# Masked copies of two chunks' score products in one instruction

## The chip, the cores and the metric

The kernel runs on one core of one Trainium2 chip, as one launch. The metric is the device time of that launch in microseconds (us), a median over several executions. The engines are called PE (TensorE, matrix products; PEld is its weight load), DVE (VectorE), ACT (ScalarE), POOL (GpSimd) and SP (SyncE, which here only issues DMAs).

## The reference, cut to what matters

Two blocks in a row. The second (a conformer convolution and a squared-relu MLP) is untouched. The first projects 1024 tokens of 1024 values, runs two kinds of gated linear attention (4 heads "G" with 256 value columns, 4 heads "H" with 128) and a cross-attention to 256 memory rows, gates the result and projects it back. The change lies in the gated linear attention:

```python
def chunked_gated_linear_attention(q, k, v, log_g):
    """Causal recurrence S_t = diag(g_t) S_{t-1} + k_t v_t^T, o_t = S_t^T q_t, chunkwise."""
    ...
    causal = jnp.tril(jnp.ones((CHUNK, CHUNK), dtype=bool))[:, :, None]
    diff = bcum[..., :, None, :] - bcum[..., None, :, :]
    decay = jnp.where(causal, jnp.exp(jnp.where(causal, diff, 0.0)), 0.0)
    scores = jnp.einsum('bhnid,bhnjd,bhnijd->bhnij', qf, kf, decay)
    o_intra = jnp.einsum('bhnij,bhnjv->bhniv', scores, vf)
    chunk_kv = jnp.einsum('bhncd,bhncv->bhndv', kf * jnp.exp(b_last - bcum), vf)
    ...
    o_inter = jnp.einsum('bhncd,nbhdv->bhncv', qf * jnp.exp(bcum), states_prev)
    return (o_intra + o_inter).reshape(b_, h_, s_, dv)
```

## The kernel before, in words

The first block works on the sequence in two halves of 512 tokens. In each half it handles 8 units (G heads singly, H heads and cross-attention heads in pairs). A unit's projections are large products on PE, split in three passes (high by high, high by low, low by high); they are the main work, and a task of them consists of groups that write the PSUM tile `ps_d`. The gated attention of a head in one half of the sequence is called a pass here; there are 16 passes (8 heads, 2 halves), all between about 70 and 1005 us. A pass has 4 chunks of 128 tokens, handled as two pairs (0, 1) and (2, 3).

For a pair `cc`, `scores(cc, half)` in `chunk_steps` makes the transposed score matrix of each chunk, a 128x128 tile `at`, from products of keys and queries at eleven levels of a binary tree: the diagonal, and blocks of 1, 2, 4, 4 columns (half 0) and of 8, 16, 16, 32, 64, 64 (half 1). Each half makes four products of 192 columns on PE: two groups `g` of operands, for each of the two chunks `m`. Before, a PSUM tile `p[m]` holds the two groups of one chunk, and the copies into `at` are made chunk by chunk in turn: `copy_predicated` takes from PSUM, where a byte mask is set, into every second block of columns. So a pair has 10 copies in half 0 and 12 in half 1, 704 in all. There are four `at` tiles, used in turn.

Then `turn(cc)` transposes the keys (`K` to `kT`), and `output(c)` multiplies a chunk's `at` with the values (in the trace `ps_m<-v,at`), adds the product of queries and state, and makes the state's update (`ps_m<-v,kT`). The steps of a pass stand in the order sc(0,0), sc(0,1), tu(0), sc(2,0), ou(0), sc(2,1), ou(1), tu(2), ou(2), ou(3). The PSUM tiles of scores (`ps_s`), of transposes and of outputs (`ps_m`) share one ring of 5 banks, so a product can wait for the bank of an earlier one.

What else is on DVE: the factors before the products (`a`, `Q`, `q`, `tree`), the low parts of the weights (`wlo`, shared with POOL by a rule in `rest`), the sums of the modulation (`macc`), and adding the output projection to the residual (`xl`).

**The order is written by a planner** while the program is built. It keeps a model of every engine's time (class `Model`), emits the groups of the big products one by one, and between two of them (`service`) emits every step that it holds to be due: whose inputs (`need`) and banks (`banks`) are ready by the model no later than PE's own modelled time plus 0.05. The model counts for each operand tile the stretch of memory it touches, so it knows which copies wait for which. Nothing is reordered at run time: each engine executes its list in order. Nearly every instruction is recorded through one helper, so its line is L217.

Of the kernel before, what the change touches and what calls it, by code (L numbers as in the profile page):

```python
# [10 lines left out]
F32 = mybir.dt.float32  # L11
# [8 lines left out]
P = 128  # L20
# [339 lines left out]
def block_kernel(ctx, tc, x, mem, w_in, w_up, w_kv, w_out, w_mod, w_pw1, w_pw2, w_dw, w_1, w_2,  # L360
# [3 lines left out]
    V, A, G, PE, DMA = [Engine(e, n, M) for e, n in ((nc.vector, "DVE"), (nc.scalar, "ACT"), (nc.gpsimd, "POOL"),  # L364
                                                     (nc.tensor, "PE"), (nc.sync, "DMA"))]
# [12 lines left out]
    def pt(tag):  # L378
        ring, bufs = BANKS[tag]
        p = ps.tile([P, 512], F32, tag=ring, name="ps_" + tag, bufs=bufs)  # L380
        M.alloc(ring, bufs, p)
        return p
# [64 lines left out]
    msk = pc.tile([P, 768], U8, name="msk")  # L447
# [1 line left out]
    lbt = pc.tile([P, 16], F32, name="lbt")  # L449
    first_only = ctx.enter_context(ExitStack())  # L450
    pb = first_only.enter_context(tc.tile_pool(name="pb", bufs=1))
    at = [pb.tile([P, P], F32, name=f"at{i}") for i in range(4)]
    for a in at:
        G.memset(a, 0.0)
    state = {}
# [214 lines left out]
    def blocks(ap, n):  # L670
        return ap.rearrange("p (b n) -> p b n", n=n)

    def factor_steps(u, j, f, req, ev):

        def up(h):
# [72 lines left out]
    n_at = [0]  # L748

    def chunk_steps(t, kind, h, u, j, f, req, ev, soon=None):  # L750
# [3 lines left out]
        st = state[kind, h]  # L754

        def scores(cc, half):
            cs = [slice(c * P, (c + 1) * P) for c in (cc, cc + 1)]
            if half == 0:
                for c in (cc, cc + 1):
                    f["at", c] = at[n_at[0] % len(at)]  # L760
                    n_at[0] += 1
            lv = ((u[f"k{j}"], u[f"q{j}"]), (f["K2"], f["Q2"])) if half == 0 else ((f["K8"], f["Q8"]), (f["K32"], f["Q32"]))
            p = [pt("s"), pt("s")]
            for m in range(2):
                for g, (ks, qs) in enumerate(lv):
                    PE.matmul(p[m][:, 192 * g:192 * (g + 1)], ks[:, cs[m]], qs[:, cc + m], start=True, stop=True)
            a = [f["at", cc], f["at", cc + 1]]
            if half == 0:
                for m in range(2):
                    V.copy_predicated(a[m], msk[:, :P], p[m][:, :P])  # L770
            col = 128 if half == 0 else 384
            for hh in (1, 2, 4, 4) if half == 0 else (8, 16, 16, 32, 64, 64):
                o = col - 384 * half
                for m in range(2):
                    V.copy_predicated(blocks(a[m], 2 * hh)[:, :, hh:], blocks(msk[:, col:col + 64], hh),
                                      blocks(p[m][:, o:o + 64], hh))
                col += 64

        def turn(cc):
            cs = [c for c in (cc, cc + 1) if not (t == NHALF - 1 and c == NT - 1)]  # L780
            p = pt("m")
            for m, c in enumerate(cs):
                PE.transpose(p[:, m * P:(m + 1) * P], f["K128"][:, c * P:(c + 1) * P], ident)
            kt = pb.tile([P, 2, P], F32, tag="kT", name="kT", bufs=2)
            A.copy(kt[:, :len(cs), :], p[:, :len(cs) * P].rearrange("p (m c) -> p m c", c=P))
            f["kT", cc], f["kT", cc + 1] = kt[:, 0, :], kt[:, 1, :]
# [27 lines left out]
        def sc(cc, half):  # L814
            names = ("K2", "Q2") if half == 0 else ("K8", "Q8", "K32", "Q32")
            return Step(lambda: scores(cc, half), lambda: [f[n] for n in names] + [f["at", c] for c in (cc, cc + 1) if half], 2)
# [954 lines left out]
    def put(name, steps, rank):  # L1771
        for st in steps:
            st.rank = rank
        lanes[name] += steps
# [4 lines left out]
    for s_, (t, (kind, h)) in enumerate(units):  # L1779
        u = us[s_]  # L1780
        if kind == "G":
            f = {}
# [10 lines left out]
        elif kind == "H":  # L1793
            for j in range(2):
                f = {}
# [6 lines left out]
        else:  # L1802
            f = [{}, {}]
            a, b = [cross_steps(u, 2 * h + j, j, f[j], [("in", s_, "q"), ("kv", 3)]) +
                    finish_steps(kind, u, j, f[j], ("mix", s_) if j else None) for j in range(2)]
# [228 lines left out]
def build(nc, arrays, dbg=None):  # L2034
    aps = [nc.dram_tensor(f"in_{n}_dram", arrays[n].shape, mybir.dt.from_np(arrays[n].dtype), kind="ExternalInput").ap()
           for n in _ARGS]
    out = nc.dram_tensor("out_0_dram", (S, D), F32, kind="ExternalOutput").ap()
    with tile.TileContext(nc) as tc:
        block_kernel(tc, *aps, out, dbg=dbg)
# [11 lines left out]
```

## Time and profile before

| what | value |
|---|---|
| median of 3 runs | 2040.17 us (2037.25 to 2045.69) |
| the profiled execution's own time | 2043.66 us |
| its span | 2041.6 us |
| PE busy | 1952.8 us, 96% |
| DVE busy | 1504.7 us, 74% |
| ACT busy | 919.5 us, 45% |
| POOL busy | 811.9 us, 40% |
| PE's mean granted clock | 0.987 of full |

How to read it: the span is the stretch from the first to the last instruction in the profile; the execution's own time is a little longer. An engine that is busy 96% of the span bounds the kernel; what the others do counts where PE waits for them. A duration in the trace runs from an instruction's start to the acknowledgement of its last write, so the instructions of one engine may overlap by a little.

### The profile page before, as it was taken

The page shows a single profiled execution, that of the slowest core. Times are in us where ns is not written, and L with a number is a line of the kernel's source. Part 1 is how long each engine was busy: PE and PEld are TensorE (multiplying, and loading weights), DVE is VectorE, ACT ScalarE, POOL GpSimd, SP SyncE. Part 2 cuts the span into 40 slices and gives each one's busy share as a digit, 9 for nine tenths or more (in the row PEclk, how much of TensorE's full clock was granted, in tenths as well). Part 3 has the DMA queues.
Part 4 walks back from the last instruction along what each step waited for, and adds up shares of the span by engine and source line. Part 5 has one row for each costly group of instructions (what it writes and reads, how often), then busy time and mean ns, then how long its engine had stood idle before and what let it go on. Part 6 is the DMA issues. An engine that isn't in the chain of part 4 may idle for free.

```text
span 2041.6 us, 29949 instructions
## 1 busy us (share of the span) xinstructions
PE 1952.8 (96%) x10892; PEld 1699.0 (83%) x10892; DVE 1504.7 (74%) x2956; ACT 919.5 (45%) x1793; POOL 811.9 (40%) x743
## 2 busy tenths in 40 slices
PE   8999999999999998999899999999999998899998
PEld 6888898789788887878789999997878886688786
DVE  5799777744667877856757676887888778777876
ACT  6433333444623334334424343335777776433343
POOL 3343334344333443343536343650000003877872
PEclk9999999999999999999999999999999999999999
DMA  5242331333123332322433232331699899776765
GB/s 198 68 159 104 114 114 63 144 124 105 45 101 136 123 109 89 133 83 83 141 133 119 71 119 91 117 132 62 179 300 270 245 263 300 264 285 263 268 250 204
DMA packets 177638, 315.05 MB, mean 154 GB/s; under 512 B 9762, under 2 KB 129442, under 8 KB 163794
## 3 DMA queue, kind: packets, MB, share of 16 engines
q1 hardware_dynamic: 175186, 309.33, 44.8%
q10 hardware_dynamic: 2304, 3.80, 0.5%
q8 instruction: 86, 1.41, 0.3%
q14 instruction: 62, 0.51, 0.1%
HBM read 241.78 MB, written 71.31 MB: 153 GB/s over the span
## 4 chain that ended last, share of the span: by engine, by line
PE 64%; DVE 20%; ACT 5%; DMA 4%; issue 3%; POOL 3%; SPq 0%; DVEq 0%; POOLq 0%; ACTq 0%
PE ps_d L217 38%; PE ps_s L217 20%; PE ps_m L217 7%; DVE macc L217 2%; DVE Q L217 2%; DVE wlo L217 2%; DMA sl<-so 1%; DVE a L217 1%; DVE at L217 1%; DVE tree L217 1%; DMA wlo<-sl 1%; DVE xn L217 1%; POOL wlo L217 1%; DVE zt L217 1%; DVE actl L217 1%
## 5 line engine op out<-in xcount | busy, mean ns | idle before, releaser
L217 POOL TENSOR_TENSOR wlo<-wst,whi 128x512 fp32r<-128x512 f32 (+1 forms) x235 | 335.9, 1444 | 393.0 <-ACT whi L217 387.9
L217 PE MATMUL ps_d<-hTh,whi 128*128 128x512 f32 x576 | 234.7, 407 | 0.0
L217 PE MATMUL ps_d<-hTh,wlo 128*128 128x512 f32 x576 | 227.8, 395 | 0.0
L217 PE MATMUL ps_d<-hTl,whi 128*128 128x512 f32 x576 | 227.5, 395 | 0.0
L217 PE MATMUL ps_d<-whi,acth 128*128 128x256 f32 x768 | 219.4, 286 | 0.5 <-DVE yg L217 0.5
L217 PE MATMUL ps_d<-wlo,acth 128*128 128x256 f32 x768 | 218.3, 284 | 1.2 <-POOL wlo L217 1.2
L217 POOL TENSOR_TENSOR wst<-wst,g 128x512 f32<-128x512 f32 x64 | 93.3, 1476 | 317.0 <-DMA g<-g2d 291.4
L217 PE MATMUL ps_d<-whi,actl 128*128 128x256 f32 x768 | 217.9, 284 | 0.0
L217 ACT CAST whi<-wst 128x1024 fp32r<-128x1024 f32 (+1 forms) x182 | 189.5, 1049 | 48.7 <-PE ps_d L217 42.9
L217 PE MATMUL ps_s<-tm,whi 128*128 128x512 f32 x620 | 191.9, 391 | 5.9 <-ACT ps_s L217 3.2
L217 PE MATMUL ps_s<-hm,tw 128*128 128x512 f32 x768 | 183.1, 393 | 5.5 <-ACT hc L217 3.4
L217 PEld LDWEIGHTS ps_s<-hm,tw 128*128 128x128 f32 x768 | 144.4, 189 | 38.5 <-ACT hc L217 5.3
L217 DVE TENSOR_TENSOR wlo<-wst,whi 128x512 fp32r<-128x512 f32 (+1 forms) x133 | 109.6, 837 | 66.4 <-ACT whi L217 63.3
L217 PEld LDWEIGHTS ps_d<-wlo,acth 128*128 128x128 f32 x768 | 148.0, 193 | 2.0 <-POOL wlo L217 1.7
L217 PEld LDWEIGHTS ps_d<-whi,acth 128*128 128x128 f32 x768 | 148.0, 193 | 1.0 <-issue 1.0
L217 PEld LDWEIGHTS ps_d<-whi,actl 128*128 128x128 f32 x768 | 148.1, 193 | 0.0
L217 PEld LDWEIGHTS ps_s<-tm,whi 128*128 128x128 f32 x620 | 115.6, 188 | 32.7 <-ACT ps_s L217 5.0
L217 DVE COPY_PREDICATED at<-msk,ps_s 128x64 f32<-128x64 uint8 (+1 forms) x704 | 109.2, 245 | 37.1 <-PE ps_s L217 37.0
L217 PEld LDWEIGHTS ps_d<-hTh,whi 128*128 128x128 f32 x576 | 110.3, 191 | 24.3 <-issue 3.3
L217 PEld LDWEIGHTS ps_d<-hTh,wlo 128*128 128x128 f32 x576 | 109.9, 191 | 24.2
L217 PEld LDWEIGHTS ps_d<-hTl,whi 128*128 128x128 f32 x576 | 110.2, 191 | 21.6 <-issue 0.2
L217 PE MATMUL ps_s<-tm,wlo 128*128 128x512 f32 x310 | 121.1, 391 | 4.6 <-DMA wlo<-sl 4.6
(290 smaller groups left out, 4995.3 us busy)
## 6 DMA issues: line engine op xcount, KB each, us to landing
wst<-in_w_in_dram SPq DMA_DIRECT2D x46, 1024.0 KB, 4.8
wst<-in_w_dram SPq DMA_DIRECT2D x32, 1024.0 KB, 6.7
sh<-so SPq DMA_DIRECT2D x112, 256.0 KB, 4.2
sl<-so SPq DMA_DIRECT2D x112, 256.0 KB, 4.0
whi<-sh SPq DMA_DIRECT2D x31, 896.0 KB, 4.8
wlo<-sl SPq DMA_DIRECT2D x31, 896.0 KB, 7.5
wm<-in_w_mod_dram SPq DMA_DIRECT2D x48, 512.0 KB, 6.8
wst<-in_w_pw_dram SPq DMA_DIRECT2D x24, 1024.0 KB, 4.9
```

The source lines that it names most:

```text
L217: r = f(*args, **kw)
```

## The change

The products of one group for both chunks now lie side by side in one bank (`p[g]`, 192 columns for each chunk), and are made group by group. The scores of both chunks of a pair lie in one tile `at` of 128 x 2 x 128; there are two such tiles instead of four single ones. `put` masks both chunks with one `copy_predicated`, the mask being read twice through a broadcast. The first copy of half 0 (the diagonal) and the blocks of 1 come from the first bank, the others of half 0 from the second; in half 1 the blocks 8, 16, 16 come from the first bank and 32, 64, 64 from the second.

```diff
--- before.py
+++ after.py
@@ -449,7 +449,7 @@
     lbt = pc.tile([P, 16], F32, name="lbt")
     first_only = ctx.enter_context(ExitStack())
     pb = first_only.enter_context(tc.tile_pool(name="pb", bufs=1))
-    at = [pb.tile([P, P], F32, name=f"at{i}") for i in range(4)]
+    at = [pb.tile([P, 2, P], F32, name=f"at{i}") for i in range(2)]
     for a in at:
         G.memset(a, 0.0)
     state = {}
@@ -670,6 +670,9 @@
     def blocks(ap, n):
         return ap.rearrange("p (b n) -> p b n", n=n)
 
+    def blocks4(ap, n):
+        return ap.rearrange("p m (b n) -> p m b n", n=n)
+
     def factor_steps(u, j, f, req, ev):
 
         def up(h):
@@ -754,27 +757,36 @@
         st = state[kind, h]
 
         def scores(cc, half):
-            cs = [slice(c * P, (c + 1) * P) for c in (cc, cc + 1)]
             if half == 0:
-                for c in (cc, cc + 1):
-                    f["at", c] = at[n_at[0] % len(at)]
-                    n_at[0] += 1
+                a = at[n_at[0] % len(at)]
+                n_at[0] += 1
+                for m in range(2):
+                    f["at", cc + m] = a[:, m, :]
+                f["at2", cc] = a
+            a = f["at2", cc]
             lv = ((u[f"k{j}"], u[f"q{j}"]), (f["K2"], f["Q2"])) if half == 0 else ((f["K8"], f["Q8"]), (f["K32"], f["Q32"]))
             p = [pt("s"), pt("s")]
-            for m in range(2):
-                for g, (ks, qs) in enumerate(lv):
-                    PE.matmul(p[m][:, 192 * g:192 * (g + 1)], ks[:, cs[m]], qs[:, cc + m], start=True, stop=True)
-            a = [f["at", cc], f["at", cc + 1]]
+            for g, (ks, qs) in enumerate(lv):
+                for m in range(2):
+                    PE.matmul(p[g][:, 192 * m:192 * (m + 1)], ks[:, (cc + m) * P:(cc + m + 1) * P], qs[:, cc + m], start=True, stop=True)
+
+            def put(dst, col, n, v, o, w):
+                mk = msk[:, col:col + n]
+                if w < n:
+                    mk, v = blocks(mk, w), blocks4(v[:, :, o:o + n], w)
+                    mk = mk.unsqueeze(1).to_broadcast([P, 2, n // w, w])
+                else:
+                    mk, v = mk.unsqueeze(1).to_broadcast([P, 2, n]), v[:, :, o:o + n]
+                V.copy_predicated(dst, mk, v)
+            v = [p[g][:, :384].rearrange("p (m t) -> p m t", m=2) for g in range(2)]
             if half == 0:
-                for m in range(2):
-                    V.copy_predicated(a[m], msk[:, :P], p[m][:, :P])
-            col = 128 if half == 0 else 384
+                put(a, 0, P, v[0], 0, P)
+            col, o = (128, 128) if half == 0 else (384, 0)
             for hh in (1, 2, 4, 4) if half == 0 else (8, 16, 16, 32, 64, 64):
-                o = col - 384 * half
-                for m in range(2):
-                    V.copy_predicated(blocks(a[m], 2 * hh)[:, :, hh:], blocks(msk[:, col:col + 64], hh),
-                                      blocks(p[m][:, o:o + 64], hh))
+                dst = blocks4(a, 2 * hh)[:, :, :, hh:] if hh < 64 else a[:, :, hh:]
+                put(dst, col, 64, v[o // 192], o % 192, hh)
                 col += 64
+                o += 64
 
         def turn(cc):
             cs = [c for c in (cc, cc + 1) if not (t == NHALF - 1 and c == NT - 1)]
```

The change moves instructions too, since the planner sees other tiles and other sizes. The number of products (PE), of ACT's and of SP's instructions stays the same; 704 copies become 352 (320 of 128 columns, 32 of 256), and seven `wlo` subtractions go from POOL to DVE. Behind some 1005 us the order is as before. Three places, the first on DVE, in the first pass, half 0 of the first pair, with what each instruction waits for (PE_49 is PE's semaphore, DVE_49 is DVE's own). Before, two tiles (`at_122`, `at_123`) in turn:

```order
L217 COPY_PREDICATED at_122<-msk,ps_s 128x128 [waits PE_49]
L217 COPY_PREDICATED at_123<-msk,ps_s 128x128 [waits PE_49]
L217 COPY_PREDICATED at_122<-msk,ps_s 128x64 [waits DVE_49]
L217 COPY_PREDICATED at_123<-msk,ps_s 128x64 [waits DVE_49]
L217 COPY_PREDICATED at_122<-msk,ps_s 128x32x2 [waits DVE_49]
L217 COPY_PREDICATED at_123<-msk,ps_s 128x32x2 [waits DVE_49]
L217 COPY_PREDICATED at_122<-msk,ps_s 128x16x4 [waits DVE_49]
```

and of the change, all on one tile:

```order
L217 COPY_PREDICATED at_122<-msk,ps_s 128x256 [waits PE_49]
L217 COPY_PREDICATED at_122<-msk,ps_s 128x128 [waits DVE_49]
L217 COPY_PREDICATED at_122<-msk,ps_s 128x64x2 [waits DVE_49,PE_49]
L217 COPY_PREDICATED at_122<-msk,ps_s 128x32x4 [waits DVE_49] x2
L217 TENSOR_TENSOR wlo<-wst,whi 128x512 [waits DMAHW4_49,Activation_49,Pool_49]
```

Half as many copies; each now waits for the one just ahead of it, where before it waited for the last but one.

The second place is on PE in the third pass: the products of half 1 of the first pair (`Q_1575,K` and `Q_1585,K`, not shown) are done, then come the transposes of K, half 0 of the second pair, and the first output. Before:

```order
L217 MATMUL ps_s<-q,k 128x192 [waits DVE_49]
L217 MATMUL ps_s<-Q_1529,K_1500 128x192
L217 MATMUL ps_d<-whi,mixh 128x512 [waits Activation_49]
...
L217 MATMUL ps_d<-whi,mixl 128x512
L217 MATMUL ps_m<-v,at_122 128x256 [waits DVE_49,Activation_49]
L217 MATMUL ps_m<-v,kT 128x256
```

and of the change:

```order
L217 MATMUL ps_s<-Q_1481,K_1437 128x192 [waits DVE_49]
L217 MATMUL ps_s<-Q_1481,K_1437 128x192
L217 MATMUL ps_m<-v,at_122 128x256 [waits DVE_49,Activation_49]
L217 MATMUL ps_m<-v,kT 128x256
L217 MATMUL ps_d<-whi,mixh 128x512
L217 MATMUL ps_d<-wlo,mixh 128x512
```

The first output has moved ahead of a group of twelve products. So it is in 12 of the 16 passes (1 to 5, 7 to 12 and 14), with a group of 12 or 24 products; in two more (13 and 15) it has moved ahead of two cross-attention scores.

The third place is on DVE in the eleventh pass, between the copies of half 0 and of half 1 of the first pair. Before:

```order
L217 COPY_PREDICATED at_123<-msk,ps_s 128x16x4 [waits DVE_49]
L217 TENSOR_SCALAR macc<-wm,scv 128x512 [waits DMAHW0_49]
L217 SCALAR_TENSOR_TENSOR macc<-wm,scv,macc 128x512 [waits DVE_49]
L217 TENSOR_TENSOR xl<-ps_d,xl 128x512 [waits DMAHW6_49,PE_49]
L217 COPY_PREDICATED at_122<-msk,ps_s 128x8x8 [waits PE_49]
```

and of the change:

```order
L217 COPY_PREDICATED at_122<-msk,ps_s 128x32x4 [waits DVE_49] x2
L217 TENSOR_SCALAR macc<-wm,scv 128x512 [waits DMAHW1_49,Pool_49]
L217 SCALAR_TENSOR_TENSOR macc<-wm,scv,macc 128x512 [waits DVE_49]
L217 SCALAR_TENSOR_TENSOR macc<-wm,scv,macc 128x512 [waits DMAHW2_49,DVE_49]
L217 SCALAR_TENSOR_TENSOR macc<-wm,scv,macc 128x512 [waits DVE_49]
L217 TENSOR_TENSOR xl<-ps_d,xl 128x512 [waits DMAHW7_49,PE_49]
L217 COPY_PREDICATED at_122<-msk,ps_s 128x16x8 [waits PE_49]
```

Two more sums of the modulation have come ahead of the copies of half 1; the second and the sixth pass show the same.

## Rows read from the trace of the kernel before

**Rows 1.** The page's busy line: us, share of the span, instructions.

```profile
PE 1952.8 (96%) x10892; PEld 1699.0 (83%) x10892; DVE 1504.7 (74%) x2956; ACT 919.5 (45%) x1793; POOL 811.9 (40%) x743
```

**Rows 2.** Busy time by stretch: length, PE, PEld, DVE, ACT, POOL, clock, DMA, GB/s.

```profile
777.70:783.50 5.80, 5.80 (x15) 4.71 (x16) 1.38 (x4) 1.93 (x8) 0.00 (x0) 0.50 0.33 137
349.50:352.30 2.80, 2.80 (x14) 2.34 (x14) 2.57 (x18) 0.71 (x1) 0.00 (x0) 1.00 0.00 0
571.98:574.40 2.42, 2.42 (x8) 2.42 (x9) 2.37 (x14) 0.00 (x0) 0.00 (x0) 0.50 0.02 7
70.00:1005.00 935.00, 896.58 (x4910) 779.68 (x4909) 667.50 (x1675) 369.33 (x816) 365.18 (x354) 0.98 0.30 107
```

**Rows 3.** PE's waits from 70 to 1005 us: total, times, longest.

```profile
PE ps_s L217 <- DVE at L217: 11.3, 4, 4.2
...
PE ps_m L217 <- DVE at L217: 2.2, 3, 1.2
```

**Rows 4.** Groups of DVE by form: busy us, mean ns, idle before.

```profile
L217 DVE TENSOR_TENSOR wlo<-wst,whi 128x512 fp32r<-128x512 f32 x129 | 105.9, 835 | 62.5 <-ACT whi L217 59.6 <-POOL K L217 3.0
L217 DVE COPY_PREDICATED at<-msk,ps_s 128x64 f32<-128x64 uint8 x640 | 97.5, 239 | 33.1 <-PE ps_s L217 33.0
...
L217 DVE COPY_PREDICATED at<-msk,ps_s 128x128 f32<-128x128 uint8 x64 | 16.3, 296 | 4.0 <-PE ps_s L217 3.9
```

**Rows 5.** DVE in order of time: start, duration, instruction; dependent and independent neighbours.

```profile
567.35 0.43 DVE L217 TENSOR_TENSOR Q<-q,a 128x256 f32<-128x256 f32 x1
567.81 0.42 DVE L217 TENSOR_TENSOR Q<-Q,tree 128x256 f32<-128x256 f32 x1
568.15 0.42 DVE L217 TENSOR_TENSOR a<-a 128x256 f32<-128x256 f32 x1
```

**Rows 6.** The fourth pass in order of time: DVE's copies, PE's products.

```profile
212.31 0.23 DVE L217 COPY_PREDICATED at<-msk,ps_s 128x64 f32<-128x64 uint8 x1 [1.89 <-PE ps_s L217]
212.97 3.16 DVE L217 COPY_PREDICATED at<-msk,ps_s 128x64 f32<-128x64 uint8 x21 [0.42 <-PE ps_s L217]
...
211.47 1.46 PE L217 MATMUL ps_s<-Q,K 128*128 128x192 f32 x8
...
213.96 0.49 PE L217 MATMUL ps_s<-Q,K 128*128 128x192 f32 x2
```

**Rows 7.** Passes 2, 3, 7 and 11: half 1's products, its first copies, a sum.

```profile
114.96 1.47 PE L217 MATMUL ps_s<-Q,K 128*128 128x192 f32 x8
116.06 0.22 DVE L217 COPY_PREDICATED at<-msk,ps_s 128x64 f32<-128x64 uint8 x1
...
164.12 1.46 PE L217 MATMUL ps_s<-Q,K 128*128 128x192 f32 x8
167.41 3.26 DVE L217 COPY_PREDICATED at<-msk,ps_s 128x64 f32<-128x64 uint8 x22
...
345.47 1.46 PE L217 MATMUL ps_s<-Q,K 128*128 128x192 f32 x8
348.79 3.28 DVE L217 COPY_PREDICATED at<-msk,ps_s 128x64 f32<-128x64 uint8 x22
...
677.68 1.46 PE L217 MATMUL ps_s<-Q,K 128*128 128x192 f32 x8
679.55 0.75 DVE L217 SCALAR_TENSOR_TENSOR macc<-wm,scv,macc 128x512 f32<-128x512 f32 x1
680.82 3.29 DVE L217 COPY_PREDICATED at<-msk,ps_s 128x64 f32<-128x64 uint8 x22
```

**Rows 8.** Waits for copies in order of time: DVE's ten copies, PE.

```profile
775.98 1.68 DVE L217 COPY_PREDICATED at<-msk,ps_s 128x128 f32<-128x128 uint8 x10
...
777.67 0.55 PE L217 MATMUL ps_s<-mkh,xqh 128*128 128x256 f32 x1 [4.19 <-DVE at L217]
...
348.09 0.41 PE L217 MATMUL ps_m<-ident,K 128*128 128x128 f32 x2 [1.16 <-DVE at L217]
...
571.98 0.98 PE L217 MATMUL ps_s<-q,k 128*128 128x192 f32 x2 [2.15 <-DVE at L217]
```

## The prediction

> **What bounds the kernel now.** The page's busy line comes first: PE works 96% of the span, DVE 74% [rows 1]. So a lighter DVE shortens nothing by itself; only PE's idle time can be won, or added to. The table by stretch then gives the stage that the change touches: from 70 to 1005 us PE is busy 896.6 of 935 us, which leaves 38.4 us idle, and DVE is busy 667.5 us [rows 2]. The table of PE's waits says how much of the 38.4 us the masked copies end: 11.3 us in four waits for banks (`ps_s`) and 2.2 us in three on `ps_m`, 13.5 us in all [rows 3]. The table of DVE's groups gives their price: 640 copies of 64 columns at 239 ns and 64 of 128 at 296 ns, 97.5 + 16.3 = 113.8 us with overlaps counted twice [rows 4]. Last the passes in order of time: when the copies start, when they end, and where PE stands then [rows 5 to 8].
>
> A difference of under 0.5% (10.2 us) is about what a measurement of this kernel cannot tell from no change.
>
> **The copies.** 704 become 352. A copy of 64 columns takes 0.23 us [rows 6] and one of 128 takes 0.296 [rows 4], so 64 columns more cost 0.066. I take 0.30 us for the new 128-column copies and 0.30 + 0.13 = 0.43 for the 32 of 256. But a duration is not a distance. In a row of 21 the old copies follow each other every 3.16 / 21 = 0.15 us [rows 6], each starting before the one ahead has ended. That works because neighbours write different tiles. In the change every copy waits for the one just ahead (the first place shown with the change). What such a wait costs is seen on DVE's factor products: one that reads its neighbour's result starts 0.03 us behind its end (567.35 + 0.43 to 567.81), one that doesn't starts 0.08 us ahead of it (567.81 + 0.42 to 568.15) [rows 5]. So a new copy comes every 0.33 us, where two old ones took 0.30.
>
> Half 0: 0.43 + 4 x 0.30 + 4 x 0.03 = 1.75 us, less 0.08 to the next instruction 1.67; the ten old ones took 1.68, less 0.08 likewise 1.60 [rows 8]. Half 1: 6 x 0.30 + 5 x 0.03 = 1.95, less 0.08 is 1.87, against 12 x 0.15 = 1.8. Over 32 pairs DVE gains nothing: 32 x (1.67 + 1.87 - 1.60 - 1.80) = +4 us. The bounds: if the new copies overlapped like the old, one every 0.22 us, half 0 and half 1 would take 1.2 and 1.3 us and DVE would save 32 x 0.9 = 29 us; if broadcast and second dimension cost as much as a second copy, 0.46 us each, it would lose another 352 x 0.13 = 46. I take the dependent rows, the nearest. Seven `wlo` subtractions at 0.835 us come to DVE [rows 4], 5.8 us more; PE's matrix work covers both, unless DVE is late at a place where PE waits. Those places are next.
>
> The Trainium skill (VectorE: DVE Perf Modes, section "The DRAIN you can't avoid") says that a semaphore behind every instruction costs nothing, because the next one cannot start ahead of the flush anyway. Rows 5 speak against it: 0.11 us lie between a dependent and an independent neighbour. By the rule the copies would overlap, which is the first rival below.
>
> **What comes free earlier.** The ten old copies of half 0 alternate between two banks, so both are held until the row is nearly over: PE's wait ended 1.69 us behind the first copy (775.98 to 777.67) [rows 8]. In the change the first bank is done after two copies, 0.43 + 0.03 + 0.30 = 0.76 us. So a bank comes 0.9 us sooner at four places (348.09, 571.98, 777.67 [rows 8] and the second wait of 4.2 us [rows 3]): 3.6 us. From the other three waits in rows 3, 13.5 - 4.2 - 4.2 - 2.15 - 1.16 = 1.8 us, I take all. Gain: 5.4 us at most.
>
> **What loses its cover.** The planner now holds half 1 to be done when half 0 of the next pair has been multiplied, since its first three copies no longer wait for the second bank. So in 12 passes the first output stands ahead of a group of products (second place shown), in two more ahead of two cross-attention scores. Take the fourth pass, where DVE waits for PE. Half 1's products start at 211.47, the first copy 0.84 us later; 0.84 + 1.95 gives the last copy's end 2.8 us behind the start. PE reaches the output when the last products are issued, 213.96 + 0.33 = 214.29, also 2.8 us behind [rows 6]. No wait, but no slack: wherever the first copy comes later than 0.84 us, PE, and with it every product queued behind the output, stands still for just that time. Before, a group of some 2.8 us lay in between and hid it.
>
> How late it is is read in four passes, first copy less start of products less 0.84 [rows 7]: second 0.26, third 2.45, seventh 2.48, eleventh 2.30 us. In the second and the eleventh two more sums of 0.75 us stand ahead of the copies (third place shown), so 1.8 and 3.8. Together 1.8 + 2.4 + 2.5 + 3.8 = 10.5 us. In the first and ninth pass something stands between the halves too (one subtraction, one addition to `xl`); for them I take 1 and 2 us, the third pass as their ceiling. The remaining passes run like the fourth: nothing. Sum 13.5 us; bounds: 4 us, if DVE catches up wherever PE stood still just before, and 25 us, if all fourteen were as late as the ones read, on average 1.8.
>
> A long wait costs twice. Behind the wait of 4.19 us the granted clock is 0.50 for the 5.8 us from 777.70, behind the one of 2.15 us for 2.4 us from 571.98, and behind the one of 1.16 us it is 1.00 [rows 2, 8]: 2.4 of TensorE's GHz fall to 1.2. Half of such a stretch is lost, 1.2 to 2.9 us. Three new waits are over 2 us, in the third, seventh and eleventh pass: 3 x 1.5 = 4.5 us, near the lower end because the products that follow are at hand; bounds 0 and 9.
>
> A rule that speaks against the change is in the Trainium skill (Perfetto Trace Analysis, section "Optimizing Scalar/DVE Operations"): where DVE isn't saturated but makes other engines wait, breaking instructions up may let work finish sooner. The old copies are such pieces, and the third pass agrees: there DVE's lateness, not its load, is what PE would meet.
>
> **The sum.** -5.4 + 13.5 + 4.5 = +12.6 us on the profiled execution's own 2043.66 us, 2056.3. That execution lies 3.5 us above the median of 2040.17, so the forecast is **2052 us**, 0.6% slower, with its own range from 2046 to 2066.
>
> **Rivals.**
>
> *The copies overlap after all (faster, 0.14).* Then a pair costs 0.9 us less on DVE. Half 1 ends 0.65 us sooner and half 0 0.5, so each of the six late passes loses 1.15 us of its wait: 13.5 - 6.9 = 6.6. Of the 13.5 us that copies cost PE now 9 go, with the clock behind them 4 more, and of the other 25 us of PE's idle time, with a DVE that is 23 us lighter, a quarter, 6. That makes 6.6 - 9 - 4 - 6 = -12 us, 2028. For it speaks the old row of 0.15 us, against it rows 5. It decides where a copy's distance is under 0.25 us.
>
> *The lateness doesn't come through (same, 0.36).* The order is another one throughout the first half of the program. A wait of PE lets DVE catch up, and the group that followed the output now covers later steps. If half of 13.5 us remains, no wait is over 2 us and the clock holds: 6.8 - 5.4 = +1.4 us, 2042. For it speaks that ten of the 16 passes aren't late.
>
> *Slower by much (inside the forecast's 0.50).* The whole of it at the upper bounds: 25 + 9 - 3 = +31 us, 2071.
>
> **Chances.** Slower 0.50, same 0.36, faster 0.14; the forecast's case reaches a little into "same", the middle rival a little into both others, which about cancel. The range that leaves out 2 in 10 runs from 2030, near the first rival, to 2066, below the far end.
>
> **What would show it.** In the changed profile the copies of 128 columns take near 0.30 us and a row of six near 2 us; DVE's busy time hardly falls. PE's waits on `at` move from `ps_s` to `ps_m` (the output) and grow from 13.5 to some 20 us, over 2 us in passes 3, 7 and 11; the granted clock dips there. The waits behind half 0 shorten by 0.9 us. From 1005 us on nothing changes. I am wrong if six copies take 1.3 us, or if the outputs show no wait although the copies are chained, or if the time moves in stretches that hold no copies.

## The result, and the profile after

The changed kernel takes 2062.52 us (median of four runs, 2061.17 to 2063.70) against 2039.47 us before (four runs in the same comparison, 2037.25 to 2045.69): ratio 1.0103, 95% interval 1.0082 to 1.0123. By the ratio it is slower by 21 us (17 to 25). Forecast were 2052 us, 0.6% slower, range 2030 to 2066: the side is right and the range holds it, the loss is about 1.7 times the forecast one.

The page's busy line of the changed kernel, against [rows 1]:

```profile
PE 1960.8 (95%) x10892; PEld 1702.1 (83%) x10892; DVE 1518.3 (74%) x2611; ACT 917.5 (45%) x1791; POOL 807.0 (39%) x734
```

DVE executes 345 instructions fewer and is busy 14 us longer. Where the time went is read by stretches of the same work. The products into `ps_d` stand in the same order among themselves in every kernel here, but for one task that changes places near 850 us, so they serve as a ruler: the first stretch runs from the first of these records to the 3901st (the first block, with all 16 passes), the second from there to nearly the end. Columns as in [rows 2]: length, PE, PEld, DVE, ACT, POOL, clock, DMA, GB/s. Before:

```profile
11.08:1036.82 1025.74, 982.06 (x5401) 853.00 (x5400) 730.94 (x1795) 413.07 (x898) 400.81 (x386) 0.98 0.31 110
1036.82:2024.34 987.52, 959.08 (x5445) 836.18 (x5444) 760.23 (x1137) 493.74 (x865) 403.05 (x333) 1.00 0.60 199
```

and after:

```profile
10.90:1055.64 1044.74, 987.62 (x5400) 852.49 (x5399) 743.44 (x1450) 410.95 (x897) 396.56 (x378) 0.98 0.31 108
1055.64:2042.29 986.65, 961.51 (x5445) 839.74 (x5443) 761.39 (x1137) 493.89 (x865) 402.50 (x333) 0.99 0.60 199
```

The second stretch is unchanged (987.5 and 986.7 us). The first grew by 19.0 us: PE is idle 57.1 us instead of 43.7 (+13.4), and the trace counts it busy 5.6 us longer for the same products.

That second part is not the clock. The granted clock is 0.98 in both rows, and the trace puts 44.4 us of this stretch at the lower of the two levels in both kernels. Behind two of the new waits shown below (2.51 and 2.98 us) the clock stays at 1.00, behind the one of 2.54 us it is 0.53 (columns as above):

```profile
78.40:84.00 5.60, 5.56 (x39) 5.44 (x40) 2.87 (x9) 1.11 (x4) 0.00 (x0) 1.00 0.54 187
123.60:129.00 5.40, 5.40 (x38) 5.27 (x39) 5.09 (x11) 2.06 (x5) 0.02 (x1) 1.00 0.02 5
702.40:705.80 3.40, 3.36 (x9) 2.85 (x10) 2.12 (x6) 0.73 (x3) 0.00 (x0) 0.53 0.02 5
```

Over the whole program the four runs of the changed kernel have a granted clock of 0.984 to 0.987, the 50 runs of the kernel before in the comparisons below 0.982 to 0.988. What the 5.6 us are is known only in part. PE comes to a stop 53 times in this stretch instead of 37; in 15 of the 16 passes the first output is now such a stop. The last product ahead of a stop is counted busy to its modelled end, 0.33 us behind its start, where products in a row start 0.16 us apart. So an estimated 16 x 0.17 = 2.7 us of waiting stand in PE's busy time. The rest stays open.

What PE waited for in the first stretch from 60 us on, after (total us, times, longest; waits of over 0.15 us):

```profile
PE ps_m L217 <- DVE macc L217: 16.2, 7, 3.4
PE ps_m L217 <- DVE at L217: 12.9, 7, 3.0
PE ps_d L217 <- DVE wlo L217: 6.0, 4, 3.1
PE ps_s L217 <- DVE at L217: 5.0, 6, 3.5
PE ps_m L217 <- DVE osb L217: 5.0, 4, 2.6
```

and the lines of before for the same stretch that aren't in [rows 3]:

```profile
PE ps_m L217 <- DVE macc L217: 7.5, 4, 3.4
...
PE ps_m L217 <- DVE orc L217: 3.0, 1, 3.0
...
PE ps_m L217 <- DVE osb L217: 2.3, 4, 0.8
```

The waits on `at` moved from `ps_s` (11.3 to 5.0) to `ps_m` (2.2 to 12.9), 13.5 to 17.9 us in all. But they are a third of what was added. The waits for the modulation's sums (`macc`) grew by 8.7 us and those for the finished outputs (`osb`, before they are transposed) by 2.7; one of 3.0 us on `orc` is gone. Together 4.4 + 8.7 + 2.7 - 3.0 = 12.8 of the 13.4 us; the others, of up to 1.1 us each way, about cancel.

Some of these waits on PE, in order of time (in brackets the wait and what ended it):

```profile
78.44 0.46 PE L217 MATMUL ps_m<-v,at 128*128 128x256 f32 x1 [2.51 <-DVE at L217]
123.59 0.45 PE L217 MATMUL ps_m<-v,at 128*128 128x256 f32 x1 [2.98 <-DVE at L217]
196.13 0.33 PE L217 MATMUL ps_m<-ident,osb 128*128 128x128 f32 x1 [2.60 <-DVE osb L217]
702.44 0.76 PE L217 MATMUL ps_m<-v,at 128*128 128x256 f32 x1 [2.54 <-DVE at L217]
801.24 0.55 PE L217 MATMUL ps_s<-mkh,xqh 128*128 128x256 f32 x1 [3.55 <-DVE at L217]
```

The first, second and fourth are the outputs that lost their cover in passes 1, 2 and 11. The last is the wait of 4.19 us in [rows 8], 0.64 us shorter.

The copies, in the groups of DVE by form (busy us, mean ns, idle before):

```profile
L217 DVE COPY_PREDICATED at<-msk,ps_s 128x128 f32<-128x128 uint8 x320 | 104.7, 327 | 36.7 <-PE ps_s L217 22.0 <-DVE at L217 0.5
...
L217 DVE COPY_PREDICATED at<-msk,ps_s 128x256 f32<-128x256 uint8 x32 | 14.0, 439 | 3.2 <-PE ps_s L217 3.2
```

Half as many copies take 118.7 us where [rows 4] has 113.8. One half 0, copy by copy, shows why the mean is 327 ns and not 300:

```profile
217.41 0.44 DVE L217 COPY_PREDICATED at<-msk,ps_s 128x256 f32<-128x256 uint8 x1 [1.35 <-PE ps_s L217]
217.88 0.45 DVE L217 COPY_PREDICATED at<-msk,ps_s 128x128 f32<-128x128 uint8 x1
218.43 0.44 DVE L217 COPY_PREDICATED at<-msk,ps_s 128x128 f32<-128x128 uint8 x1
218.91 0.29 DVE L217 COPY_PREDICATED at<-msk,ps_s 128x128 f32<-128x128 uint8 x1
219.24 0.29 DVE L217 COPY_PREDICATED at<-msk,ps_s 128x128 f32<-128x128 uint8 x1
```

The second and third, with blocks of 1 and 2 columns, take 0.45 us, those with 4 and more columns 0.29. Each copy starts behind the end of the one ahead, by 0.03 to 0.10 us. So half 0 takes 2.13 us (forecast 1.75, old 1.68), half 1 2.03 (forecast 1.95, old 1.8).

Three things are mixed in the result: other copies, another layout of the banks, and another order of all engines. The experiments take them apart. All ratios below are to the kernel before, run on the same chip in the same comparison, in five rounds; there are three such comparisons, and the ratio 1.0103 of the changed kernel comes from a fourth.

### The profile page after: what moved, and what is told of

Same layout as the page of the kernel before. It is cut to its first block, busy times and chain, and to the rows that moved or that the text cites. A ratio compares the mean times of both kernels' runs of the same rounds, so it can differ in the third digit from the quotient of the medians.

```text
span 2059.2 us, 29642 instructions
## 1 busy us (share of the span) xinstructions
PE 1960.8 (95%) x10892; PEld 1702.1 (83%) x10892; DVE 1518.3 (74%) x2611; ACT 917.5 (45%) x1791; POOL 807.0 (39%) x734
## 3 DMA queue, kind: packets, MB, share of 16 engines
q1 hardware_dynamic: 175186, 309.33, 44.4%
## 4 chain that ended last, share of the span: by engine, by line
PE 61%; DVE 23%; ACT 4%; DMA 4%; issue 4%; POOL 3%; SPq 0%; DVEq 0%; POOLq 0%; ACTq 0%
PE ps_d L217 34%; PE ps_s L217 20%; PE ps_m L217 7%; DVE Q L217 3%; DVE macc L217 3%; DVE a L217 2%; DVE at L217 2%; DVE wlo L217 2%; POOL wlo L217 1%; DMA sl<-so 1%; DVE tree L217 1%; DVE xn L217 1%; DMA wlo<-sl 1%; ACT whi L217 1%; DVE zt L217 1%
## 5 line engine op out<-in xcount | busy, mean ns | idle before, releaser
L217 POOL TENSOR_TENSOR wlo<-wst,whi 128x512 fp32r<-128x512 f32 (+1 forms) x228 | 330.1, 1463 | 395.6 <-ACT whi L217 389.3
L217 DVE COPY_PREDICATED at<-msk,ps_s 128x128 f32<-128x128 uint8 (+1 forms) x352 | 117.2, 337 | 39.8 <-PE ps_s L217 25.2
```

Of the source, the lines that this page charges most:

```text
L217: r = f(*args, **kw)
```

## The experiments

### New copies in the old order

The planner's model is told the old products and copies (and takes the two halves of an `at` tile for two tiles), while the new ones are issued:

```diff
 class Engine:
-            if op != "memset":
+            if op != "memset" and not self.model.mute:
                 self.model.note(self.name, op, args, kw)
...
         def scores(cc, half):
+            M.mute = True
...
+            M.mute = False
+            for m in range(2):
+                for g, (ks, qs) in enumerate(lv):
+                    M.note("PE", "matmul", (p[m][:, 192 * g:192 * (g + 1)], ks[:, cs[m]], qs[:, cc + m]), {})
...
+                for m in range(2):
+                    M.note("DVE", "copy_predicated", (blocks(b[m], 2 * hh)[:, :, hh:], blocks(msk[:, col:col + 64], hh),
+                                                      blocks(p[m][:, o:o + 64], hh)), {})
```

The lists of all engines are then those of the kernel before, but for the copies and, within a half's four products, which comes first.

> The changed kernel's merged copies, but its planner is told the old copies, so every engine's list is the one of the kernel before, copies apart. My theory (two causes together: copies that take longer than the planner thinks, and an order with no slack behind them): with the cover of a group of products back in front of the first output, the waits on v,at fall from 12.9 us to under 2, the macc waits from 12.9 to under 7, and the time is within 0.5% of before, 2034 to 2050 us. Rival 1 (the slower copies alone cost it, in any order): half 0 still takes 2.1 and half 1 2.0 us, the lateness meets PE elsewhere, and 2055 to 2063 us remain. Rival 2 (the order alone costs it): below before by the 5 us that earlier banks give, 2030 to 2037 us, with half 0's bank waits shortened by 0.9 us each.

Measured: 2036.96 us, ratio 0.9966 (0.9954 to 0.9979): 7 us faster than before. The first stretch:

```profile
11.06:1029.80 1018.74, 976.45 (x5401) 846.59 (x5400) 737.90 (x1443) 413.15 (x898) 402.39 (x385) 0.99 0.32 111
```

The same copies that stand in the kernel at 1.0103 cost nothing here; PE is idle 42.3 us and busy 976.5. They are as long as there (half 0 2.13 us), and DVE is busy 7 us longer than before. From these 1018.74 to the 1044.74 us of the changed kernel it is 26.0 us, 14.8 idle and 11.2 in products, and nothing differs but the order and the engine of seven `wlo` subtractions (140 on DVE in the changed kernel, 133 here). Part of the 11.2 is the clock: 27.3 us of this stretch are at the lower level here, 44.4 in the changed kernel, which makes 8.5 us at most. The first rival, that the slower copies cost it in any order, has fallen. The time lies in the ranges of both other theories; the next run tells them apart.

### Old copies in the new order

The reverse: the old products and copies are issued, on views of the new `at` tile, and the model is told the new ones.

> The old products and copies (one chunk each, 0.13 to 0.2 us apart), in the order of the changed kernel: its planner is told the merged copies. My theory: half 0 ends 0.45 us and half 1 0.24 us sooner than with merged copies, so each of the seven waits on v,at loses some 0.7 us; 12.9 us become about 8, macc waits stay near 8 to 10; 2046 to 2056 us. Rival 1 (the slower copies alone): 2036 to 2044 us, v,at waits under 3 us. Rival 2 (the order alone): 2057 to 2065 us, v,at and macc waits near 12 us each as in the changed kernel.

Measured: 2059.58 us, ratio 1.0081 (1.0066 to 1.0095); the first stretch is 1039.14 us. The time is that of the theory "the order alone", the waits only in part:

```profile
PE ps_m L222 <- DVE macc L222: 14.4, 7, 3.4
PE ps_s L222 <- DVE at L222: 7.3, 5, 4.2
...
PE ps_m L222 <- DVE at L222: 6.7, 6, 2.1
PE ps_m L222 <- DVE osb L222: 4.6, 4, 2.3
```

With copies that end sooner the outputs wait 6.7 instead of 12.9 us, but `macc` and `osb` wait nearly as in the changed kernel. So of the loss to before some 16 us come with the order and the old copies. The 4 to 5 us beyond it, for the merged copies and the new layout of the banks together, are no more than the two intervals leave open.

### The layout of the banks alone, in the old order

The new products, but one copy for each chunk, in turn, and the model told the old ones as above:

```diff
...
-                put(dst, col, 64, v[o // 192], o % 192, hh)
+                for m in range(2):
+                    s = 192 * m + o % 192
+                    V.copy_predicated(blocks(a[:, m, :], 2 * hh)[:, :, hh:], blocks(msk[:, col:col + 64], hh),
+                                      blocks(p[o // 192][:, s:s + 64], hh))
```

> One part of the change alone: products of a group side by side in a bank, but one copy for each chunk (in turn, so a copy doesn't wait for its neighbour), in the order of the kernel before. My theory of the gain (a bank is done after four copies, 0.7 us, where it was done after nine, 1.6 us): the four waits for banks fall from 11.3 to 7.5 us, the clock dips behind them shorten, 2032 to 2038 us. Rival (the second bank is what PE waits for, or the wait moves to the next step): 2038 to 2044 us, no change. Third: over 2044 us, if the copies of two chunks from one bank meet each other and take longer than 0.15 us apart.

Measured: 2032.14 us, ratio 0.9942 (0.9927 to 0.9956), as the theory of the gain has it. It beats both kernels. The waits for banks fell to 8.6 us (forecast 7.5); the first stretch is 1012.65 us, PE busy 974.28: of the 13.1 us to before 5.3 are idle time and 7.8 products, of which far more ran at the full clock (23.9 us of the stretch are at the lower level, 44.4 before).

### Merged copies that don't wait for each other

The changed kernel in its own order, with every second copy into a tile that nobody reads, which leaves half of the score blocks out of the result:

```diff
-                V.copy_predicated(dst, mk, v)
+                M.note("DVE", "copy_predicated", (dst, mk, v), {})
+                M.mute = True
+                V.copy_predicated(real, mk, v)
+                M.mute = False
...
+                dst, real = [blocks4(x, 2 * hh)[:, :, :, hh:] if hh < 64 else x[:, :, hh:] for x in (a, a if i % 2 else spare)]
```

> The changed kernel with its order, but every second masked copy writes a spare tile that nobody reads, so that neighbours write different tiles; this leaves half of the score blocks out of the result. My theory (the wait for the copy just ahead sets the distance): copies of 128 columns come 0.2 to 0.22 us apart instead of 0.33, half 1 takes 1.3 instead of 2.03 us, half 0 1.5 instead of 2.13; the v,at waits fall from 12.9 to 4 us or less; 2036 to 2048 us. Rival (a copy of 128 columns occupies DVE for its whole 0.30 us, broadcast and second dimension set it): 0.30 us apart, half 1 1.85 us, v,at waits above 10 us, 2055 to 2062 us.

Measured: 2047.83 us, ratio 1.0022 (1.0010 to 1.0033). A half 1 there, copy by copy:

```profile
216.60 0.30 DVE L218 COPY_PREDICATED spare<-msk,ps_s 128x128 f32<-128x128 uint8 x1 [2.61 <-PE ps_s L218]
216.81 0.30 DVE L218 COPY_PREDICATED at<-msk,ps_s 128x128 f32<-128x128 uint8 x1
217.00 0.30 DVE L218 COPY_PREDICATED spare<-msk,ps_s 128x128 f32<-128x128 uint8 x1
217.25 0.30 DVE L218 COPY_PREDICATED at<-msk,ps_s 128x128 f32<-128x128 uint8 x1
217.46 0.29 DVE L218 COPY_PREDICATED spare<-msk,ps_s 128x128 f32<-128x128 uint8 x1
217.65 0.30 DVE L218 COPY_PREDICATED at<-msk,ps_s 128x128 f32<-128x128 uint8 x1
```

Durations are the same 0.30 us, distances 0.2 instead of 0.33. So it is the wait for the neighbour, and not the width, that sets the distance. The Trainium skill (VectorE: DVE Perf Modes, section "The DRAIN you can't avoid") has it that a semaphore behind each instruction costs nothing extra; here the wait for the copy just ahead costs 0.13 us a copy. Waits on `v,at` fell from 12.9 to 4.5 us and the first stretch by 17 us, to 1027.78. In the new order DVE's lateness does count, then: 0.7 us less for each half brings back most of the loss, while in the old order the same lateness cost nothing.

### The cover given back

If the first output without cover were the cause, holding it would do:

```diff
         r[0].req, r[5].ev = req, ev
+        r[4].pad = 1.0
...
-        return max([done[r] for r in st.req] + [M.time(*st.need()) if st.need else 0.0] + banks(st.psum))
+        return max([done[r] for r in st.req] + [M.time(*st.need()) + st.pad if st.need else 0.0] + banks(st.psum))
```

> The changed kernel with one rule added to its planner: the first output of a pass is held 1 us longer by the model, which puts it behind the group of products again in all 12 passes (and behind the cross-attention scores in two); merged copies and everything else stay as the planner chooses. Of the 26 us between the changed kernel and the one with merged copies in the old order, 12.2 are waits on v,at, and some 11 are products that run longer at a lower clock. My theory now (the lost cover is the main cause): v,at waits under 1 us, half of the clock's share comes back too, 2036 to 2048 us where before has 2042. Rival (the rest of the order, macc and osb waits, 16 and 5 us, carry it): 2050 to 2060 us.

Measured: 2056.95 us, ratio 1.0070 (1.0050 to 1.0089). My theory was wrong here and the rival right: only 7 us come back (1.0103 to 1.0070, little more than the two intervals leave open), though the group of products stands ahead of the output again in all 12 passes. PE's waits:

```profile
PE ps_m L217 <- DVE macc L217: 13.7, 7, 3.4
PE ps_s L217 <- DVE at L217: 8.1, 6, 3.5
...
PE ps_m L217 <- DVE stG L217: 5.9, 4, 2.3
PE ps_m L217 <- DVE osb L217: 4.7, 4, 2.3
```

The waits on the outputs are gone but for 1.8 us in the sixth pass, where no cover had been lost. In their place PE waits for the state's update (`stG`, which stands behind the copies on DVE): in the second pass 2.30 us there instead of 2.98 at the output. A wait that is taken away at one meeting of PE and DVE comes back at the next as long as DVE is late. The seven `wlo` subtractions on DVE aren't the cause either: here DVE has 132 of them, fewer than in the old order. Why it is late in the second pass stands on DVE ahead of half 1's copies. Before:

```profile
114.87 0.48 DVE L217 TENSOR_SCALAR macc<-wm,scv 128x512 f32<-128x512 f32 x1
115.39 0.75 DVE L217 SCALAR_TENSOR_TENSOR macc<-wm,scv,macc 128x512 f32<-128x512 f32 x1
116.06 0.22 DVE L217 COPY_PREDICATED at<-msk,ps_s 128x64 f32<-128x64 uint8 x1
```

and in the changed kernel (here with the cover held it is the same, 3.22 us):

```profile
117.78 0.48 DVE L217 TENSOR_SCALAR macc<-wm,scv 128x512 f32<-128x512 f32 x1
118.30 3.21 DVE L217 SCALAR_TENSOR_TENSOR macc<-wm,scv,macc 128x512 f32<-128x512 f32 x3
121.43 0.28 DVE L217 COPY_PREDICATED at<-msk,ps_s 128x128 f32<-128x128 uint8 x1
```

Two sums more, and one of the three takes over 1.6 us instead of 0.75. The first copy comes 2.7 us later against its products than before (3.81 us behind their start at 117.62, 1.10 before).

### Thin sums: is it what stands ahead of the copies?

Three kernels with the sums behind the first (84 by the trace; the 77 below is my miscount) cut to 16 columns, without a change in the order, which leaves most of the modulation out of the result: the changed kernel, the new copies in the old order, and the one with the cover held.

```diff
-                    V.scalar_tensor_tensor(acc, w, c, acc, op0=ALU.mult, op1=ALU.add)
+                    M.note("DVE", "scalar_tensor_tensor", (acc, w, c, acc), {})
+                    M.mute = True
+                    V.scalar_tensor_tensor(acc[:, :16], w[:, :16], c, acc[:, :16], op0=ALU.mult, op1=ALU.add)
+                    M.mute = False
```

> The changed kernel, order unchanged, with the 77 later modulation sums (macc) 16 columns wide instead of 512; this leaves most of the modulation out of the result. It takes some 55 us of DVE's work away, of it the sums that stand between copies in passes 2, 6, 7 and 11. Compared with the next run (same copies, old order, same thin sums): full-width the two are 26 us apart. If the sums that stand ahead of copies make the rest of the loss (what holding the cover doesn't give back), the distance falls to 4 to 12 us, this one at 2030 to 2042. If the sums' places don't matter, it stays 18 to 26 us, this one at 2044 to 2056.

> Merged copies in the old order, with the same thin sums (most of the modulation left out). Its waits on macc (7.6 us to 1030 us, one more of 3.4 behind) go, and the clock dips behind them: 2022 to 2032 us against 2037 with full sums, by either theory. If DVE's load as a whole doesn't matter outside of the macc waits, 2028 to 2034.

> The changed kernel with the first output held behind its group, and thin sums (most of the modulation left out). With full sums it stands 20 to 23 us behind the old order. If sums ahead of copies are the second cause, both causes are gone here and it stands within 6 us of the old order with thin sums, 2024 to 2038 us. If other moves in the order carry the loss, it stays 15 us or more behind it, 2040 to 2052 us.

Measured, with the same copies in all six (the thin ones in one comparison, the full ones in three; loss is the difference of the ratios to the old order's, times 2042 us; idle is length less PE's busy time in the first stretch):

| order | full sums: ratio, loss | thin sums: ratio, loss | idle full, thin |
|---|---|---|---|
| old | 0.9966, 0 | 0.9877 (0.9862 to 0.9892), 0 | 42.3, 28.2 |
| planner's own (the change) | 1.0103, 28 us | 0.9959 (0.9946 to 0.9971), 17 us | 57.1, 39.6 |
| own, cover held | 1.0070, 21 us | 0.9940 (0.9928 to 0.9953), 13 us | 55.7, 36.2 |

The old order with thin sums is faster than I had put it by either theory (2018.67 us). The distance of the changed kernel lies between the two expectations: the sums that stand in PE's and the copies' way carry 8 to 11 us of the loss, the lost cover 4 to 7, and 13 us remain with both gone. By its two intervals each loss of the table can be off by 4 to 5 us, so by the times alone the cover's share is not shown. The lengths of the first stretch in the six profiles give 26.0 and 22.8 us for the losses with full sums, 16.5 and 10.5 with thin ones; that makes 9.5 to 12.3 us for the sums, 3.2 to 6.0 for the cover and 10.5 for the remainder. In the second pass the account closes. There the changed kernel loses 3.7 us against the old order (1.3 of them are given back right behind) and the one with the cover held 3.0; with thin sums they lose 1.0 and 0.0 (lengths of the same stretch of products). The remainder lies in several places that I had not looked at, of which the largest are 2.9 us in the sixth pass and 1.8 and 4.0 us where PE meets `osb`, the second with the clock's part in it. What moved DVE's instructions there was not tried one by one.

### The planner told better prices

If the planner went wrong because it counts a merged copy at 0.20 us, it can be told what the trace shows:

```diff
+        if op == "copy_predicated":
+            narrow = out.ap[-1][0] != 1 or out.ap[-1][1] < 4
+            return 0.13 + n / 900.0 + (0.18 if narrow else 0.0)
```

> The changed kernel, whose planner is told what the merged copies take by the trace: 0.27 us and its dependence of 0.06 for 128 columns, 0.45 for blocks of 1 and 2 columns, 0.41 for 256 (it had 0.20, 0.20 and 0.34). The covers are back in all passes. Theory (the planner's price, not the copy, is what went wrong): v,at waits under 1 us, near the kernel with merged copies in the old order, 2034 to 2044 us where before has 2042. Rival (any order that isn't the old one meets other waits, since the planner is off elsewhere too): 2046 to 2060 us.

Measured: 2041.84 us, ratio 0.9999 (0.9989 to 1.0009). The covers are back and the waits on `v,at` gone, inside my range, and 21 us of the loss are back (1.0103 to 0.9999); but it doesn't reach the 0.9966 of the same copies in the old order, and `macc` still waits 15.8 us. Next, the sums' price alone:

```diff
+        if op == "scalar_tensor_tensor" and out.tensor.name.startswith("macc"):
+            return 0.15 + n / 960.0
```

> The changed kernel, whose planner is told what a modulation sum (macc) takes, 0.74 us from one to the next by the trace instead of 0.60; the first output stays ahead of the group of products in 12 passes. If the macc sums that stand too early are a cause of their own, the macc waits fall from 12.9 to under 7 us and the time by 6 to 12 us, to 2050 to 2058. If the lost cover carries nearly all, v,at waits stay at 10 to 14 us and the time at 2057 to 2066 us.

Measured: 2057.07 us, ratio 1.0073 (1.0054 to 1.0093), between the two. The waits on `macc` halved (16.2 to 8.3 us), those on `v,at` stayed (13.9), and other outputs now meet late copies: the wait in the third pass grew from 1.06 to 2.97 us, and the seventh, which had none, has one of 3.08.

The same price on the fastest kernel:

> The fastest so far (products of a group side by side, one copy for each chunk, planner told the old copies) with the modulation sums priced at 0.74 us instead of 0.60. If a planner with truer prices makes fewer waits, macc waits fall from 7.5 to under 4 us and the time from 2032 to 2026 to 2030 us; rival: the waits only move, 2030 to 2036 us.

Measured: 2033.72 us, ratio 0.9956 (0.9940 to 0.9972), against 0.9942 without: no gain, as the rival has it. Last, the fastest kernel's instructions in the order that the planner makes when it is told just them:

> Products of a group side by side, one copy for each chunk, and the planner told just that; it puts the first output ahead of the group in 14 passes by itself. Same instructions as the fastest kernel so far (0.9942 of before in the old order), only the order differs, and its copies are neither chained nor misjudged by the planner. If the order costs by itself, 2048 to 2062 us; if it costs only with copies that end later than planned, 2030 to 2040 us.

Measured: 2041.24 us, ratio 0.9996 (0.9987 to 1.0005), just above the second expectation's range. The planner's price for these copies (0.14 us for 64 columns) is near their distance in the trace (0.13 to 0.2), they don't wait for each other, and against 0.9942 the order still costs 0.54%, 11 us: the first output meets late copies five times (0.57 to 2.12 us each).

## Why the prediction was right or wrong

**Side and range: right**, and the rival that the copies overlap has fallen: 0.33 us apart when each waits for its neighbour, 0.2 when not. Its condition (under 0.25 us) was well put: where the copies did overlap, 17 of the first stretch's 19 us came back. But even then the time did not fall below before.

**The copies: mechanism right, size too small.** Distances of 0.33 us came as worked out from [rows 5]. Missed was that copies of 128 columns with blocks of 1 and 2 columns take 0.45 us, not 0.30: half 0 takes 2.13 us, not 1.75. That DVE is not what bounds the kernel by its load was right: in the old order the longer copies cost nothing.

**Banks that come free earlier: right in size, in part by luck, -5.4 forecast, -7 measured** (new copies in the old order, interval -4 to -9). The way differs: PE's waits on `at` fell by 3.1 us only (`ps_s` from 11.3 to 9.7, `ps_m` from 2.2 to 0.7; the wait of 4.19 us by 0.64, not 0.9, since half 0's first two copies take longer), its idle time by 1.4, and 5.6 us are products. The granted clock of that kernel is 0.989 on the mean of its runs, against 0.985 before, which makes an estimated 7 us of 2040. The clock's gain behind shorter waits was not in my sum.

**The lost cover: 13.5 us forecast, 12.9 measured** as waits on `v,at`. That the total fits is luck, for by place it is worse: pass 3 1.06 (forecast 2.4), pass 7 none (2.5), pass 6 1.79 (none forecast), pass 1 2.51 (1), pass 2 2.98 (1.8), pass 11 2.54 (3.8). And giving the cover back gave 4 to 7 us. A wait counted at the place where PE meets DVE is not what disappears when that place is moved.

**The clock: 4.5 forecast, none measured** against before. Of the longer waits at the first outputs the clock falls behind those in passes 6 and 11, but not behind the ones in passes 1 and 2; elsewhere some of the old stretches at the lower level are gone and new ones have come, and together they last 44.4 us of the first stretch in both kernels. In its place PE is counted busy 5.6 us longer, for the reasons given with the rows above, as far as they are known.

**The step that failed** is "The remaining passes run like the fourth: nothing", and with it the limit of the whole sum to waits on `at` and the clock behind them. I saw that two more sums stood ahead of the copies and priced them by what they do to the output behind them. I did not ask what else the same rearranged list makes late: the transposes and products that read the sums (+8.7 us) and the finished outputs (+2.7). Forecast against measured, in the first stretch: waits on `at` +8.1 and +4.4; all other waits 0 and +9.0 (13.4 - 4.4); clock +4.5 and 0; PE's other busy time 0 and +5.6; sum +12.6 and +19.0. What the sum had, it had 8.2 us too high; what it lacked, 14.6 us, is more than the whole difference. So that the range holds the result is luck in part. (The forecast itself is 2052.8 by its sum, put down as 2052.) That nothing changes behind 1005 us was right.

The rival "the lateness doesn't come through" failed for the same reason: DVE does catch up at some places (pass 7), but a planner's new order brings new meetings.

## What to carry to other kernels

When a planner writes the order, an edit to one instruction is an edit to the whole order: run the edit in the old order first, and the old instructions in the new order, before judging either. A wait is removed by making the late engine earlier; giving it cover at one meeting sends much of it to the next. And fewer instructions are not less time when each now waits for its neighbour: two tiles in turn let short copies start every 0.13 us and copies of twice the width every 0.20, one tile makes the wide ones line up every 0.33.

## What I had not expected of the hardware

Blocks of one or two columns are dear: old copies of 64 columns took 0.30 us with blocks of 1 and 2 columns and 0.22 with 4 and more, the new ones of 128 columns 0.45 and 0.30.

A sum of 512 columns takes 0.75 us on DVE, and up to 1.88 us where POOL was subtracting low parts when its turn came; no run changed this alone. The kernel with the cover held, on DVE:

```profile
116.99 0.75 DVE L217 SCALAR_TENSOR_TENSOR macc<-wm,scv,macc 128x512 f32<-128x512 f32 x1
...
118.56 1.65 DVE L217 SCALAR_TENSOR_TENSOR macc<-wm,scv,macc 128x512 f32<-128x512 f32 x1
```

and on POOL:

```profile
117.92 3.45 POOL L217 TENSOR_TENSOR wlo<-wst,whi 128x512 fp32r<-128x512 f32 x2 [7.40 <-ACT whi L217]
```

Of 84 such sums 13 take over 1.2 us before, 14 after and 20 with the cover held; POOL works during 80% or more of their time on average, during 12 to 18% of the others'. POOL pays too: its two subtractions took 3.45 us here, and 2.52 in the old order. This agrees with the Trainium skill (SBUF — State Buffer, section "SBUF: two separate sides"), by which a DVE instruction with two inputs in SBUF and a GpSimd instruction that reads SBUF lock each other out for a whole instruction.
